# A hybrid attention layer on one core: token places by residue modulo 16, and far blocks of pattern 16 transposed in place

## The chip, the core and the metric

One core of one Trainium2 chip runs the whole layer. The metric is device time in microseconds (us) from start to end of one execution. Besides the timed runs there is one execution taken by the hardware profiler; the rows shown further down come from it. TensorE (PE) multiplies matrices and transposes 128x128 blocks, VectorE (DVE) and ScalarE (ACT) work on elements, GpSimd (POOL) as well but not on PSUM, and SyncE (SP) issues all transfers from one queue, in order.

## What is computed

x has 2048 tokens of 1024 channels. The layer normalises x, projects it with `w_in` (1024 x 4096), runs two groups of channels, and projects their gated outputs back:

```python
h = rmsnorm(x, norm_pre_g)
z = jnp.einsum('bsd,de->bse', h, w_in)
q, k, v, g_attn, c_h, c_b, c_c, g_conv = jnp.split(z, cuts, axis=-1)
...
for window, dilation in ((128, 1), (512, 4), (2048, 16)):
    o_i, lse_i = dilated_window_attn(q, k, v, window, dilation)
...
mix_w = jax.nn.softmax(jnp.stack(lses, axis=0), axis=0)
attn_out = sum(mix_w * outs) * jax.nn.silu(g_attn)
conv_out = c_b * causal_depthwise_conv(c_c * c_h, conv_w) * jax.nn.silu(g_conv)
y = jnp.einsum('bse,ed->bsd', concat(attn_out, conv_out), w_out)
x = x + rmsnorm(y, norm_post_g)
```

There are 12 attention heads of 64 channels, with rotary q and k. Each has three patterns: the last 129 keys, every 4th key back to 512, every 16th key back to 2048, each query seeing 129 keys of a pattern at most. The convolution group has 256 channels and three taps.

## The kernel before

**Stages.** Tokens come in four chunks of 512 (b = 0 to 3). `x_chunk` transposes x on TensorE against an identity, splits the result into a high and a low part (every large product is three matmuls: high x high, high x low, low x high; L848 to L850), and writes it to DRAM. Then 32 units follow, 8 groups of projection columns times 4 chunks: a convolution unit for group 0 and for group 7, and in between `attn_unit` for six pairs of heads (p = 0 to 5). After them the output product takes 8 quarters of 256 tokens, each with 7 forms and 7 products (L1008 to L1010) of a Strassen scheme.

**Places on chip.** A chunk's 512 tokens lie by residue modulo 4: place = 128 r + j for token 4 j + r. `KK` holds the keys as 4 residues x all chunks. Pattern 4 and pattern 16 are computed together, as "kind 4": for a residue r, 128 queries against the keys of the same residue in all chunks up to b (`score4`, L631). In the chunks b - 1 and b a mask takes both patterns; in the chunks before those (the far blocks, c < b - 1) only keys of the same residue modulo 16 count, every 4th of a block, and the mask sets all others to a probability of zero. Pattern 1 is "kind 1": four blocks of 128 consecutive tokens per chunk (`score1`, L659), for which the queries are copied to token order (`Q1`, GpSimd L582) and the keys are read in runs of 32.

**From scores to outputs.** VectorE adds the mask and takes the minimum in one pass out of PSUM (L638, L666), ScalarE takes the exponential and the row sums (L642, L670). A product with v needs keys on partitions, so `probs` transposes the probabilities, four blocks at a time: TensorE into a PSUM bank of ring `st` (L684), ScalarE copies the high part to `pt` (L689), VectorE subtracts for the low part (L690), and TensorE multiplies with v (L703). `gather` adds the halves of the outputs. Row sums of kind 1 go through DRAM (`ed`) to change their order; so does v (`vd`), for kind 1. The two kinds' mixing weights go through DRAM too (`ad`, L788, then broadcast back to `ab`, L791) and multiply the outputs (L807, L808, GpSimd L809).

**What sets the order.** Every operation is handed to a planner (`Plan`) with a duration, a priority and its reads and writes. The planner runs through time, gives each engine the ready operation of lowest priority number, hands out the slots of rings, and emits the instructions of each engine in the order so found. Each engine works its list strictly in that order. It allows for a delay between engines: a long one before TensorE uses another engine's result, a short one between ScalarE and VectorE.

**The output product.** `mixed` loads 128 tokens of one residue modulo 4, 4 x 128 channels, from DRAM; `sums` adds such tiles; `form` splits the sum into a high part (ScalarE, L976) and a low part (VectorE, L977), 56 times each. In `x_chunk`, token order in a chunk was set once, by loading rows 4 apart; `store` writes rows 4 apart.

## Time and profile before

| What | Value |
|---|---|
| Median of 3 runs | 1218.33 us (1218.25 to 1221.13) |
| The profiled execution | 1222.89 us, span 1220.8 us |
| TensorE busy | 1201.8 us, 98% of the span |
| VectorE busy | 916.0 us, 75% |
| ScalarE busy | 717.9 us, 59% |
| GpSimd busy | 260.1 us, 21% |
| Granted TensorE clock | 0.994 |
| One pair of heads, steady | 141 us |

The span is from the first to the last instruction of the profiled execution, whose own time is 2.1 us longer. In rows by line, "L690 DVE TENSOR_TENSOR pt<-st,pt 128x512 ... x204 | 136.1, 686 | 46.8 <-ACT ..." reads: line, engine, operation, what it writes and reads, shapes, count, total busy us, mean ns of one, then the idle time just before them and who ended it. PEld is the loading of the stationary operand, which overlaps PE. A matmul's mean there is its latency through the pipe, so the spacing of matmuls is read from the chain of waits instead, where "829.17 0.87 PE st L684 x8" is a start, a length and a count. Rows that give three durations (673/696/1770) are minimum, median and maximum in ns.

### The profile page before, as it was taken

Reading aid. Unit: us, or ns where it says so; the run is one execution under the profiler, and the core shown is the slowest. Engines: PE = TensorE matmul, PEld = TensorE weight load, DVE = VectorE, ACT = ScalarE, POOL = GpSimd, SP = SyncE. Lnnn points to the kernel's source line nnn. Section 1 sums busy time; section 2 is a strip of 40 time slices with the busy share of each in tenths; the row PEclk is TensorE's granted clock in tenths of the full one; section 3 lists DMA queues with packets and bytes.
Section 4 is the critical chain, followed back from the end, with each engine's and each line's share of the span. In section 5 each row is a group of like instructions: output and inputs, shape, how many; then the busy total and the mean of one; then the engine's idle time right before and its main releaser. Section 6 shows DMA issues by size and latency. Waiting matters only on the chain.

```text
span 1220.8 us, 20955 instructions
## 1 busy us (share of the span) xinstructions
PE 1201.8 (98%) x6856; PEld 993.4 (81%) x6856; DVE 916.0 (75%) x2287; ACT 717.9 (59%) x1874; POOL 260.1 (21%) x212
## 2 busy tenths in 40 slices
PE   8999999999999999999999999999999999999997
PEld 6888888888878888788887888788888888777886
DVE  5556477877777787787788867787877759988876
ACT  6533447767557676576667676486676553454443
POOL 0011123322322232222332223222323113000000
PEclk9999999999999999999999999999999999999999
DMA  9989777766777657766877748767678779555452
GB/s 342 343 317 338 269 232 236 234 205 200 240 252 245 205 182 261 240 184 209 260 223 254 243 119 269 232 234 248 199 233 280 213 229 302 174 163 175 136 181 86
DMA packets 155884, 280.39 MB, mean 230 GB/s; under 512 B 31872, under 2 KB 90368, under 8 KB 155776
## 3 DMA queue, kind: packets, MB, share of 16 engines
q1 hardware_dynamic: 155776, 279.06, 69.6%
q8 instruction: 54, 0.88, 0.3%
q14 instruction: 54, 0.44, 0.1%
HBM read 215.36 MB, written 51.05 MB: 218 GB/s over the span
## 4 chain that ended last, share of the span: by engine, by line
PE 84%; DVE 8%; DMA 3%; ACT 2%; issue 1%; SPq 1%; DVEq 0%; ACTq 0%
PE z L848 16%; PE z L850 16%; PE z L849 16%; PE st L703 8%; PE st L684 7%; PE st L631 4%; PE st L659 3%; PE st L1010 2%; PE st L1008 2%; PE st L1009 2%; DMA rp<-rp 1%; PE z L1008 1%; PE z L1010 1%; PE z L1009 1%; ACT p L642 1%
## 5 line engine op out<-in xcount | busy, mean ns | idle before, releaser
L848 PE MATMUL z<-xt,w 128*128 128x512 f32 x960 | 397.1, 414 | 0.0
L850 PE MATMUL z<-xt,w 128*128 128x512 f32 x960 | 377.7, 393 | 0.0
L849 PE MATMUL z<-xt,w 128*128 128x512 f32 x960 | 376.4, 392 | 0.0
L850 PEld LDWEIGHTS z<-xt,w 128*128 128x128 f32 x960 | 180.5, 188 | 40.3
L848 PEld LDWEIGHTS z<-xt,w 128*128 128x128 f32 x960 | 181.2, 189 | 32.7 <-issue 3.4
L849 PEld LDWEIGHTS z<-xt,w 128*128 128x128 f32 x960 | 181.5, 189 | 25.8
L690 DVE TENSOR_TENSOR pt<-st,pt 128x512 fp32r<-128x512 f32 x216 | 142.3, 679 | 48.1 <-ACT pt L689 46.2
L642 ACT ACTIVATE p<-p,sm 128x128 f32<-128x128 f32 (+3 forms) x192 | 105.9, 555 | 73.2 <-DVE sm L638 72.9
L689 ACT CAST pt<-st 128x512 fp32r<-128x512 f32 x216 | 120.0, 579 | 36.0 <-PE st L684 34.1
L703 PEld LDWEIGHTS st<-pt,v 128*128 128x128 f32 x852 | 121.5, 190 | 18.2 <-DVE pt L690 4.9
L703 PE MATMUL st<-pt,v 128*128 128x256 f32 x852 | 133.1, 287 | 2.0 <-DVE pt L690 1.9
L684 PE MATMUL st<-cst,p 128*128 128x128 f32 x852 | 123.1, 275 | 2.4 <-DVE sm L638 1.0
L723 DVE TENSOR_TENSOR uu<-st,uu 64x256 f32<-64x256 f32 x192 | 80.0, 421 | 57.1 <-ACT uu L722 53.5
L684 PEld LDWEIGHTS st<-cst,p 128*128 128x128 f32 x852 | 100.6, 141 | 22.8 <-issue 3.2
L752 POOL TENSOR_TENSOR uu<-uu 128x512 f32<-128x512 f32 x48 | 72.4, 1509 | 209.1 <-DVE uu L723 207.4
L638 DVE CUSTOM_DVE_ANT_0 p<-st,cst 128x128 f32<-128x128 f32 (+3 forms) x192 | 81.8, 487 | 46.7 <-PE st L631 46.4
L721 ACT COPY uu<-st 64x256 f32<-64x256 f32 x192 | 70.2, 368 | 58.7 <-PE st L703 52.3
L670 ACT ACTIVATE p<-p,e 128x256 f32<-128x256 f32 (+1 forms) x192 | 94.9, 499 | 12.4 <-DVE e L666 12.3
L562 POOL TENSOR_TENSOR rp<-rp,cs 128x512 f32<-128x512 f32 x24 | 35.3, 1472 | 225.7 <-DMA rp<-rp 145.4
L666 DVE CUSTOM_DVE_ANT_0 p<-st,cst 128x256 f32<-128x256 f32 (+1 forms) x192 | 66.8, 411 | 20.5 <-PE st L659 20.4
L562 DVE TENSOR_TENSOR rp<-rp,cs 128x512 f32<-128x512 f32 x72 | 55.9, 791 | 23.4 <-DMA rp<-rp 23.0
L722 ACT COPY uu<-st 64x256 f32<-64x256 f32 x192 | 69.6, 367 | 3.2 <-DVE uu L723 0.4
(320 smaller groups left out, 1842.7 us busy)
## 6 DMA issues: line engine op xcount, KB each, us to landing
xt<-xt SPq DMA_DIRECT2D x256, 512.0 KB
cs<-t SPq DMA_DIRECT2D x28, 768.0 KB
raw<-in_w_in SPq DMA_DIRECT2D x59, 256.0 KB
rp<-rp SPq DMA_DIRECT2D x192, 64.0 KB
vd<-v SPq DMA_DIRECT2D x96, 128.0 KB
v<-vd SPq DMA_DIRECT2D x24, 512.0 KB
ab<-ad SPq DMA_DIRECT2D x48, 256.0 KB
mix<-g SPq DMA_DIRECT2D x32, 256.0 KB
```

The source lines that it names most:

```text
L562: add(e, dur, pr, lambda o=o, a=a, i=i, eng=eng: eng.tensor_tensor(o.ap, a.ap, cs.ap[:, i], op=ALU.mult), r=[cs], w=[o], port=True)
L638: add("DVE", dvet(w) + 0.01, pr + URG, lambda h=h, r=r, P4=P4: vec.tensor_tensor_reduce(P4.ap[:, r, 0:w], ps[h].ap[:, (r - r0) * w:(r - r0 ...
L642: add("ACT", actt(w) + 0.19, pr, lambda h=h, r=r, P4=P4: act.activation(P4.ap[:, r, 0:w], P4.ap[:, r, 0:w], AF.Exp, bias=s4(0, h)[:, r:r + ...
L670: add("ACT", actt(256 - lo[g]) + 0.19, pr, lambda h=h, g=g, P1=P1: act.activation(P1.ap[:, g, lo[g]:], P1.ap[:, g, lo[g]:], AF.Exp, bias=E ...
L684: nc.tensor.transpose(ps.ap[:, i * 128:(i + 1) * 128], pp.ap[:, a, c * 128:(c + 1) * 128], ident)
L689: add("ACT", actt(m * 128, True), pr + URG, lambda: act.copy(pt.ap[:, :m, 0, :], p4()), r=[ps], w=[(pt, 0)])
L690: add("DVE", dvet(m * 128), pr + URG, lambda: vec.tensor_tensor(pt.ap[:, :m, 1, :], p4(), f(pt.ap[:, :m, 0, :]), op=ALU.subtract), r=[ps, ...
L703: mm(dst, v, pt.ap[:, i], start=s, stop=e)
L723: add("DVE", dvet(256), pr + URG, lambda: vec.tensor_tensor(cols(a, lo), o()[lo:lo + 64, 0], cols(a, lo), op=ALU.add), r=[O], w=[(a, (h, h ...
L848: mm(z.ap, w.ap[:, 0, js], xt.ap[:, 0], start=kt == 0, stop=False)
L849: mm(z.ap, w.ap[:, 0, js], xt.ap[:, 1], start=False, stop=False)
L850: mm(z.ap, w.ap[:, 1, js], xt.ap[:, 0], start=False, stop=kt == KT - 1)
```

## The change

A chunk's place is now 128 r + 32 s + a for token 16 a + 4 s + r: within a residue modulo 4, the places of one residue modulo 16 are 32 neighbours. In `x_chunk` the rows of x are loaded as before, and TensorE transposes against a permuted identity (`perm`) that puts the tokens in these places. The tables, masks, shifts of the convolution and all views follow. `KK` is 16 residues x all chunks; `score4` reads it in runs of 32, `score1` in runs of 8. `Q1`, v and E reach the token order of pattern 1 (now a permuted one within its 128) by other views and transfers, of the same count for v and E. The mixing weights take four transfers to `ad` instead of one. The forms of the output product put the tokens back in order: `cells` reads them with a step of 32 elements (L976 and L977, then L1009 and L1010).

In a far block, queries and keys of one residue modulo 16 are now a 32x32 square on the diagonal, and everything else is zero. VectorE's transpose turns each 32x32 square of a tile in place, which for such a block is the whole transpose. So `probs` becomes `parts` and `times`: the far blocks are transposed by VectorE in place (L699), copied by ScalarE and subtracted by VectorE (L701) out of SBUF into `pt`, without TensorE and PSUM; the other blocks go as before. `times` multiplies all blocks of half the outputs in one go.

```diff
-    order = np.arange(C).reshape(128, 4).T.reshape(-1)
+    order = np.arange(C).reshape(32, 4, 4).transpose(2, 1, 0).reshape(-1)
...
+    perm = np.ascontiguousarray(ident[place].T)
...
-                    nc.tensor.transpose(ps.ap[:, i * 128:(i + 1) * 128], xn[i].ap[:, kt * 128:(kt + 1) * 128], ident)
+                    nc.tensor.transpose(ps.ap[:, i * 128:(i + 1) * 128], xn[i].ap[:, kt * 128:(kt + 1) * 128], perm)
...
-        add("DVE", 0.25, pe, lambda: vec.tensor_copy(u.ap[:, 0:2, 1:], u.ap[:, 4:6, 0:127]), r=[(u, 1)], w=[(u, 2)])
+        add("DVE", 0.25, pe, lambda: vec.tensor_copy(u.ap[:, 0:2, 32:], u.ap[:, 4:6, 0:96]), r=[(u, 1)], w=[(u, 2)])
+        add("DVE", 0.15, pe, lambda: vec.tensor_copy(u.ap[:, 0:2, 1:32], u.ap[:, 4:6, 96:127]), r=[(u, 1)], w=[(u, 3)])
...
-                               KK[j][lo:lo + 64, r, 0:w], start=x == 0, stop=x == 2)
+                               KK[j][lo:lo + 64, 4 * r:4 * r + 4, 0:w // 4].rearrange("p s (c a) -> p c s a", a=32), start=x == 0, stop=x == 2)
...
-                            keys = kk[:, :, k0 + 32:k0 + 64] if lo[g] else kk[:, :, k0:k0 + 64].rearrange("p r (c j) -> p c r j", c=2)
+                            keys = kk[:, :, k0 + 8:k0 + 16] if lo[g] else kk[:, :, k0:k0 + 16].rearrange("p x (c a) -> p c x a", c=2)
...
+        def parts(h, kind, blk, far=False):
+            pt, m, pp = Tok(pt_r), len(blk), P[h, kind]
+            tiles = sorted({a for a, _ in blk})
+            if far:
+                def src():
+                    return pp.ap[:, tiles[0]:tiles[-1] + 1, 0:(b - 1) * 128]
+                def dst(l):
+                    return pt.ap[:, :m, l].rearrange("p (a c) q -> p a c q", c=b - 1)
+                def cut(a):
+                    return a.rearrange("p a (c q) -> p a c q", q=128)
+                add("DVE", dvet(m * 128) + 0.05, pr, lambda: vec.transpose(src(), src()), w=[(pp, a) for a in tiles])
+                add("ACT", actt(m * 128), pr + URG, lambda: act.copy(dst(0), cut(src())), r=[(pp, a) for a in tiles], w=[(pt, 0)])
+                add("DVE", dvet(m * 128), pr + URG, lambda: vec.tensor_tensor(dst(1), cut(src()), f(dst(0)), op=ALU.subtract),
+                    r=[(pp, a) for a in tiles] + [(pt, 0)], w=[(pt, 1)], port=True)
...
+                if kind == 4 and b > 1:
+                    where = {}
+                    for half in range(2):
+                        rs = range(2 * half, 2 * half + 2)
+                        if b == 3 or half == 0:
+                            where.update(parts(h, 4, [(r, c) for r in (rs if b == 3 else range(4)) for c in range(b - 1)], True))
+                        where.update(parts(h, 4, [(r, c) for r in rs for c in (b - 1, b)]))
+                        times(h, 4, {ac: v for ac, v in where.items() if ac[0] in rs}, O[half])
...
-        add("DMA", 0.5, pr, lambda: nc.sync.dma_start(
-            ad.rearrange("c g f -> g c f"), ar.ap.rearrange("p a b -> p (a b)")), r=[ar], w=[ak], land=2.0)
+        for r in range(4):
+            add("DMA", 0.5, pr, lambda r=r: nc.sync.dma_start(
+                ad[:, r].rearrange("c s a -> s c a"), ar.ap[:, r]), r=[ar], w=[ak + (r,)], land=2.0)
...
-    add("DMA", 0.5, -158.5, lambda: nc.sync.dma_start(ident, consts[:, 0:128]), w=["cst"])
+    add("DMA", 0.5, -158.5, lambda: nc.sync.dma_start(cst[:, 0:256], consts[:, 0:256]), w=["cst"])
...
-            return m.ap.rearrange("p a c -> p (a c)").rearrange("p (e l t) -> p e l t", e=4, l=2)[:, :, l]
+            return m.ap.rearrange("p a c -> p (a c)").rearrange("p (e l a s) -> p e l a s", e=4, l=2, s=4)[:, :, l]
...
-            return t.ap.rearrange("p (e t) -> p e t", e=4)
+            return t.ap.rearrange("p (e s a) -> p e a s", e=4, s=4)
```

The planner finds a new order for all engines. Two places carry the prediction, both in chunk 3 of a pair of heads. On TensorE, p = 2, the first blocks of probabilities that are multiplied with v (`v_171` to `v_174` are the four chunks' v, `pt` the split probabilities, `p_182` and `p_183` the probabilities of the two heads, `cst` the identity). Before:

```order
L703 MATMUL st_118<-pt_190,v_173 128x2x128
L684 MATMUL st_117<-cst,p_182 128x128 x4
L684 MATMUL st_121<-cst,p_183 128x128 x4
L703 MATMUL st_119<-pt_191,v_174 128x2x128
L703 MATMUL st_119<-pt_191,v_171 128x2x128
L703 MATMUL st_119<-pt_191,v_172 128x2x128
```

Now:

```order
L668 MATMUL st_119<-kk_167,q_170 128x256
L730 MATMUL st_117<-pt_189,v_174 128x2x128
L730 MATMUL st_117<-pt_189,v_171 128x2x128
L730 MATMUL st_117<-pt_191,v_172 128x2x128
L730 MATMUL st_117<-pt_191,v_173 128x2x128
```

One half of a head's outputs is now multiplied in one run, its far blocks out of `pt_189`, its near ones out of `pt_191`, after the scores of pattern 1; the transposes between such runs are half as many. On VectorE, p = 1, the masks of pattern 4 and 16 (L638, now L647, each followed by the reading of its minimum) and what follows. Before:

```order
L638 ISA p_182,sm_162<-st_120,cst 128x512
L638 ISA sm_162 128x1
L638 ISA p_183,sm_162<-st_118,cst 128x512
L638 ISA sm_162 128x1
L690 TENSOR_TENSOR pt_189<-st_121,pt_189 128x4x128
L690 TENSOR_TENSOR pt_190<-st_119,pt_190 128x4x128
```

Now:

```order
L647 ISA p_183,sm_162<-st_120,cst 128x512
L647 ISA sm_162 128x1
L699 STREAM_TRANSPOSE p_182<-p_182 128x2x256
L699 STREAM_TRANSPOSE p_183<-p_183 128x2x256
L701 TENSOR_TENSOR pt_189<-p_182,pt_189 128x4x128
L647 ISA p_182,sm_162<-st_118,cst 128x512
```

The transposes stand in VectorE's queue ahead of the masks of the next scores, and they wait for ScalarE's exponentials of the same tiles. In the whole program TensorE has 708 transposes of probabilities where it had 852. After the last product with v, 222 projection matmuls stand before the first matmul of the output product where 192 stood.

More of the change, by code (lines that the diff above doesn't have):

```diff
@@ L582, in attn_unit @@
             add("POOL", poolt(C) / 2, pr, lambda l=l: pool.tensor_copy(
-                Q1.ap[:, l].rearrange("p (g r j) -> p g r j", g=4, r=4), Q.ap[:, l].rearrange("p (r g j) -> p g r j", g=4, r=4)),
+                tokens(Q1.ap[:, l]), rows(Q.ap[:, l])),
                 r=[(Q, l)], w=[(Q1, l)])
@@ L696, in pv, with times @@
+        def times(h, kind, where, O):
+            def pv():
+                for (a, c), (pt, i) in sorted(where.items()):
+                    dst = O.ap.rearrange("p (l q) -> p l q", l=2)[:, :, (a % 2) * 128:(a % 2 + 1) * 128]
                     if kind == 4:
@@ L704, in probs @@
             vs = [V2[p * NB + c] for c in range(b + 1)] if kind == 4 else [V1[p * NB + c] for c in range(max(b - 1, 0), b + 1)]
-            for half in range(2):
-                part = [(i, ac) for i, ac in enumerate(blk) if ac[0] // 2 == half]
-                if part:
-                    attn_last.append(add("PE", mmt(256) * len(part), pr, lambda part=part: pv(part), r=[(pt, 0), (pt, 1)] + vs, w=[O[half]]))
+            attn_last.append(add("PE", mmt(256) * len(where), pr, pv,
+                                 r=[(pt, l) for pt in {pt for pt, _ in where.values()} for l in range(2)] + vs, w=[O]))
         UU = {}
@@ L745, in attn_unit @@
                 O = [Tok(st_r), Tok(st_r)]
-                for i in range(0, len(bl), 4):
-                    probs(h, kind, bl[i:i + 4], O)
+                if kind == 4 and b > 1:
[6 more added lines that the diff above has]
+                        times(h, 4, {ac: v for ac, v in where.items() if ac[0] in rs}, O[half])
+                else:
+                    for i in range(0, len(bl), 4):
+                        where = parts(h, kind, bl[i:i + 4])
+                        for half in range(2):
+                            part = {ac: v for ac, v in where.items() if ac[0] // 2 == half}
+                            if part:
+                                times(h, kind, part, O[half])
                 for half in range(2):
```

99 lines of the change are left out of this document (46 added, 53 removed).

## Prediction, made before the changed kernel ran

> **What bounds the kernel now.** I read the first part of the page, then the busy time by stage, then the waits of TensorE.
>
> ```profile
> span 1220.8 us, 20955 instructions
> PE 1201.8 (98%) x6856; PEld 993.4 (81%) x6856; DVE 916.0 (75%) x2287; ACT 717.9 (59%) x1874; POOL 260.1 (21%) x212
> ```
>
> A busy share can hide matmuls that merely wait in the pipe, so the stages come next: one pair of heads in the steady middle (750 to 891 us), the change to the output product (1010 to 1100), the output product itself (1100 to 1200). The columns are length, then busy time and instructions of PE, PEld, DVE, ACT, POOL, then granted clock and DMA share.
>
> ```profile
> 750.00:891.00 141.00, 140.13 (x874) 116.76 (x875) 110.81 (x296) 93.68 (x263) 39.11 (x32) 1.00 0.71 226
> 1010.00:1050.00 40.00, 40.00 (x178) 33.13 (x177) 39.11 (x67) 14.02 (x25) 8.84 (x6) 1.00 0.76 254
> 1050.00:1100.00 50.00, 47.60 (x195) 36.79 (x194) 43.39 (x87) 24.39 (x51) 2.95 (x2) 0.97 0.52 171
> 1100.00:1200.00 100.00, 99.74 (x428) 79.75 (x427) 82.18 (x175) 45.30 (x102) 0.00 (x0) 1.00 0.48 159
> ```
>
> And what TensorE waited for, in the attention stage (125 to 1010 us) and after it, with total, count and longest:
>
> ```profile
> PE st L703 <- DVE pt L690: 1.9, 1, 1.9
> ...
> PEld st L703 <- DVE pt L690: 4.9, 10, 2.3
> ...
> PE st L1008 <- ACT xt L976: 1.8, 1, 1.8
> PE z L1010 <- DVE xt L977: 0.6, 1, 0.6
> PE z L1008 <- ACT xt L976: 0.3, 1, 0.3
> ```
>
> TensorE's queue is the kernel's clock. Nothing in attention holds it for longer than these few microseconds of 885, so a TensorE instruction taken out there is taken out of the time, as long as the other engines keep up. VectorE is next: 110.8 of 141 us per pair of heads, 82 of 100 in the output product, 39 of 40 just before that.
>
> **What the change takes away.** TensorE transposed every 128x128 block of probabilities. The change takes the far blocks of pattern 16 off it: per head 4 in chunk 2 and 8 in chunk 3, so 12 x 2 heads x 6 pairs = 144 of the 852 instructions of L684. The mean of 275 ns in the grouped rows is latency in the pipe; what a transpose costs the queue is in the chain:
>
> ```profile
> L684 PE MATMUL st<-cst,p 128*128 128x128 f32 x852 | 123.1, 275 | 2.4 <-DVE sm L638 1.0 <-DVE e L666 0.7 <-ACT p L642 0.6
> ...
> 829.17 0.87 PE st L684 x8
> 830.05 0.47 PE st L703 x4
> ...
> 830.75 0.23 PE z L849
> ```
>
> 0.87 / 8 = 0.109 us, and 144 x 0.109 = 15.7 us. The products with v (L703, 852) and the scores stay as many as they were. This is the whole gain, 2.6 us for each pair of heads.
>
> **What it adds in attention.** 36 groups of four blocks now go VectorE transpose, ScalarE copy, VectorE subtract. Rows for their prices:
>
> ```profile
> L785 DVE STREAM_TRANSPOSE t<-pa 128x128 f32<-128x128 f32 x24 | 7.5, 312 | 0.8
> L690 DVE TENSOR_TENSOR pt<-st,pt 128x512 fp32r<-128x512 f32 x204 | 136.1, 686 | 46.8 <-ACT pt L689 45.0
> L690 DVE TENSOR_TENSOR pt<-st,pt 128x384 fp32r<-128x384 f32 x12 | 6.6, 552 | 1.3 <-ACT pt L689 1.1
> L573 DVE TENSOR_TENSOR kk<-rp,kk 128x512 fp32r<-128x512 f32 x24 | 19.4, 810 | 0.0
> ```
>
> The trace has the transpose at 128 elements only. At 512 it lies between 0.686 (a two-input operation of that size) and 4 x 0.312 = 1.25 us; growing like L690, by (686 - 552) / 128 = 1.05 ns an element, it is 0.312 + 384 x 0.00105 = 0.72, which I take, the row of the operation itself carried on at the slope of its neighbour. 36 x 0.72 = 25.8 us. The subtract now reads two operands in SBUF; L573, which does that and meets GpSimd, shows 0.810 for 0.686: 36 x 0.124 = 4.5 us. Together 30.3, or 5.0 per pair of heads: VectorE goes from 110.8 in 141 to 115.8 in 138.4 us, 84%. So VectorE stays off the bound on average, and the cost is waits. The present chain (transpose on TensorE, copy, subtract) shows 1.9 + 4.9 us over 216 groups, 0.031 each. The new one crosses between ScalarE and VectorE three times instead of once, and a transpose that waits for a late exponential holds all that is queued behind it on VectorE, the mask operations (L638) of the next scores among them. I take double, 0.063 x 36 = 2.3 us given back. The bounds are 0 and, if the longer first step shows each time, 36 x (0.72 - 4 x 0.109) = 10.2.
>
> Edits that I cost at little: the scores' keys. Before, the first pattern's scores read runs of 32 elements, pattern 16's whole rows; with equal columns (chunk 1, 256) they took the same:
>
> ```profile
> 317.97 1.63 PE st L631 x24
> ...
> 323.22 1.64 PE st L659 x24
> ```
>
> So breaking rows into 32s is free for TensorE; runs of 8 I take as free too (a rival below). VectorE likewise reads runs of 32 as it reads whole rows (L807 against L808, below). The multiplications that now run over whole rows therefore gain nothing. The weights' way to DRAM is four transfers instead of one:
>
> ```profile
> L788 SPq DMA_DIRECT2D ad<-t x24: 583/592/660, 168.3 to 1013.8; - x24
> ...
> DVE uu L807 <- DMA ab<-ad: 1.4, 1, 1.4
> ...
> L807 DVE TENSOR_TENSOR uu<-uu,ab x24: 673/696/1770, 179.0 to 1027.1; 128x512 f32<-128x512 f32 x24
> L808 DVE TENSOR_TENSOR uu<-uu,ab x24: 674/682/1780, 183.4 to 1030.5; 128x512 f32<-128x512 f32 x24
> ```
>
> Three issues more put the weights back by at most 3 x 0.59 = 1.8 us, and move every later transfer in SyncE's queue by as much. L807 waited once in 24, so other work covers it; with that cover gone, VectorE would idle 24 x 1.8 = 43 us, 7 per pair of heads out of its 22.6 idle, still no TensorE term. The round trips of v and E keep five transfers each. Eight more short copies in the convolution cost under 8 x 0.28 us of VectorE (row L512). The first constants to load double, and TensorE's wait for them may grow by up to itself; I take 0.2 us.
>
> ```profile
> L512 DVE COPY u<-u x8: 278/282/286, 40.1 to 1053.5; 128x254 f32<-128x254 f32 x8
> ...
> PE st L442 <- DMA cst<-in_consts: 0.5, 1, 0.5
> ```
>
> **What it adds in the output product.** The 56 forms (8 quarters x 7) read their tokens back in natural order: the innermost step goes from 1 to 32 elements, in the copy (L976) and the subtract (L977). No row has that at this size. The nearest are 8-element operations: L769, L770 and L778 step 4 elements in one source, L771 and L779 are the same kinds without a step.
>
> ```profile
> L977 DVE TENSOR_TENSOR xt<-uu,xt x33: 677/686/694, 1046.0 to 1203.4; 128x512 fp32r<-128x512 f32 x33
> ...
> L769 DVE TENSOR_TENSOR sm<-ex,sm x24: 149/168/1252, 163.9 to 1010.1; 128x8 f32<-128x8 f32 x24
> L770 DVE TENSOR_TENSOR sm<-sm,ex x24: 171/174/1289, 164.1 to 1010.4; 128x8 f32<-128x8 f32 x24
> L771 DVE TENSOR_TENSOR sm<-sm,sm x24: 151/158/1273, 165.2 to 1011.5; 128x8 f32<-128x8 f32 x24
> L778 DVE TENSOR_TENSOR sm<-sm,ex x24: 154/168/599, 167.0 to 1012.5; 128x8 f32<-128x8 f32 x24
> L779 DVE TENSOR_TENSOR sm<-sm,sm x24: 152/155/1279, 167.0 to 1012.5; 128x8 f32<-128x8 f32 x24
> ...
> 1050.00:1100.00 50.00, 10.07 (x15) 0.97 0.52 171
> 1100.00:1200.00 100.00, 24.58 (x37) 1.00 0.48 159
> ```
>
> The last two rows are L977 alone by stage, 37 in the 100 us of the output product. By medians the step costs up to 174 - 158 = 16 ns over 8 elements, 2.0 ns each or 1.02 us a form; by minima the three pairs differ by -2 (L769 to L771), 20 and 2, a mean of 0.83 ns each or 0.43 us; the least is nothing. I take 0.43. VectorE's slack is 17.8 us over 37 forms, 0.48 each. So VectorE would be 98% busy and TensorE still sets the pace, barely. What an in-order queue loses at that load: nothing if all the slack can be used, 56 x 0.1 = 5.6 us if a fifth of it can't; I take the middle, 2.8. ScalarE has 55 of 100 us free and covers its own copies. The step before is safer: 15 forms (1050 to 1100) add 6.5 us to VectorE, which had 6.6 idle there, and by the instruction order 222 projection matmuls instead of 192 now stand between the last product with v and the first output matmul, 30 x 0.23 = 6.9 us more for VectorE's backlog. That could also remove the 2.7 us of waits after 1010; I leave that to the low end.
>
> The Trainium skill's "Vector Engine (DVE) Microarchitecture Reference" (5.2, Measured stream behaviour on trn2) speaks against this edit: a port streams at full rate only over runs of at least two adjacent words, and one source that hops every element takes 1.73 ns a column for 1.054. An estimate from that page is 0.35 us more a form, inside the slack, and the sum would be the same or up to 2.8 us better. No run here shows its rate at 512 elements.
>
> **The sum.** -15.7 + 2.3 + 0.2 + 2.8 = -10.4 us. The profiled execution took 1222.9 us (span 1220.8 and 2.1 around it), 4.6 above the median of 1218.33; on it the sum gives 1212.5, and on the median 1207.9.
>
> **Rivals.** First, VectorE becomes the bound of the output product (slower). Place: L977, 56 times. If a stepped element costs the 2.0 ns of the medians, a form takes 1.02 us more, 0.54 above the slack: 56 x 0.54 = 30 us, in place of the 2.8. -15.7 + 2.3 + 0.2 + 30 = +17, 1235. It cancels the gain from 0.48 + 13.2 / 56 = 0.72 us more a form, that is L977 at 1.4 us. For it: the medians. Against it: two of three minima show nothing. Chance that it takes over at all 0.22, half of it past the point of no gain.
>
> Second, attention waits take the place of the transposes: 10.2 for 2.3 us gives -2.5, 1215.8. For it: VectorE already waits 45 us for the copy before L690. Against it: TensorE lost only 0.031 us a group through that. Chance 0.12.
>
> Third, the first pattern's scores slow down: 576 matmuls read runs of 8. The chain's 1.64 us for 24 is 0.068 each; at twice that, 576 x 0.068 = 39 us more, 1247. Against it: 32-element runs cost nothing. Chance 0.05.
>
> Fourth, the transposes were not on the path at all: no change, about 1218. TensorE's rows speak against it. Chance 0.05.
>
> **The numbers.** The forecast keeps 0.56. Low end: no cost anywhere and the 2.7 us of waits gone, 1218.3 - 15.7 - 2.7 = 1199.9, so 1200. High end: forms at 0.74 us more, 56 x 0.26 = 14.6, and 2.3 and 0.2, +1.4 or 1219.7, and a little of what lies beyond: 1221. About 0.3% (3.7 us) is what a measurement of this kernel can tell from no change. Faster by more: 0.56, 0.11 of the first rival and 0.03 of the second, 0.70. Within it: 0.02 of the first, 0.09 of the second, 0.05 of the fourth, 0.16. Slower: 0.09 and 0.05, 0.14.
>
> **What would show it.** Right: 708 transposes on TensorE at 0.109 us in the chain, a pair of heads in some 138.8 us, 36 VectorE transposes near 0.72, the form subtract near 1.1, TensorE still over 99% in the middle of the output product. Wrong: TensorE waiting for VectorE in chunks 2 and 3, L977's successor above 1.4 us with VectorE full from 1100 on, or 24 score matmuls of the first pattern well over 1.64.

## The result, and the profile after

The changed kernel takes 1229.29 us (median of 6 runs, 1224.77 to 1231.03) where the kernel before takes 1218.58 beside it (6 runs, 1216.28 to 1221.13): a ratio of 1.0079, 95% interval 1.0058 to 1.0100, so 0.8% slower. 1207.9 was forecast, and 1229.29 lies outside the range of 1200 to 1221. The profiled execution took 1226.19 us, 3.1 below the median of its kernel (that of before was 4.3 above); sums are therefore made from medians here, and profiles only show where. All times here are of executions whose mean granted clock was 0.979 or more; one execution, of the kernel below whose planner knows the longer durations, had 0.653 and took 1670 us, and is left out.

The page of the changed kernel:

```profile
span 1224.4 us, 20804 instructions
PE 1193.9 (98%) x6712; PEld 985.3 (80%) x6712; DVE 945.4 (77%) x2331; ACT 747.1 (61%) x1874; POOL 263.0 (21%) x212
```

TensorE has its 144 instructions less, and the span is longer all the same. Where, the stages tell, in the same stretches as in the prediction:

```profile
750.00:891.00 141.00, 139.05 (x848) 115.60 (x847) 109.93 (x301) 95.04 (x264) 38.49 (x32) 0.99 0.74 222
1010.00:1050.00 40.00, 39.06 (x171) 31.54 (x170) 34.16 (x49) 18.72 (x27) 11.09 (x7) 1.00 0.64 202
1050.00:1100.00 50.00, 44.55 (x181) 34.26 (x180) 41.27 (x75) 28.07 (x45) 0.00 (x0) 0.97 0.44 143
1100.00:1200.00 100.00, 92.23 (x390) 72.09 (x389) 85.26 (x163) 56.73 (x94) 0.00 (x0) 1.00 0.41 138
```

The pair of heads looks as forecast: by the first scores of kind 4 (L640), the four steady pairs from 288.9 to 845.5 us took 139.2 us each. In the output product (last row) TensorE does 390 matmuls where it did 428, and is idle for 7.8 us of 100. The grant of its clock is full there, and no engine is full either. The first matmul of the output product and the last start of the same group, before:

```profile
L1008 PE MATMUL st<-kk,xt x14: 389/394/505, 1051.5 to 1194.2; 128*128 128x512 f32 x14
```

and after:

```profile
L1041 PE MATMUL st<-kk,xt x12: 393/395/694, 1039.6 to 1197.4; 128*128 128x512 f32 x12
```

So the changed kernel reaches the output product 11.9 us earlier, and has lost all of it, and more, by the eighth quarter. Attention gained; the output product gave it back.

The parts of the change, in the groups of the changed kernel's instructions:

```profile
L730 PEld LDWEIGHTS st<-pt,v 128*128 128x128 f32 x852 | 117.5, 190 | 13.6 <-DVE pt L714 2.3 <-issue 1.1 <-DVE pt L701 1.0
...
L1009 ACT CAST xt<-uu 128x512 fp32r<-128x512 f32 x36 | 40.3, 1140 | 34.1 <-DVE uu L930 32.1 <-PE z L882 1.9
L1010 DVE TENSOR_TENSOR xt<-uu,xt 128x512 fp32r<-128x512 f32 x36 | 39.8, 1113 | 17.0 <-ACT xt L1009 17.0
L668 PE MATMUL st<-kk,q 64*128 64x256 f32 x540 | 44.9, 308 | 3.4 <-DVE sm L647 3.4
L701 DVE TENSOR_TENSOR pt<-p,pt 128x512 fp32r<-128x512 f32 x36 | 25.5, 707 | 1.1
L699 DVE STREAM_TRANSPOSE p<-p 128x512 f32<-128x512 f32 x36 | 24.2, 697 | 8.4 <-ACT p L651 8.4
```

and in its chain, in attention:

```profile
315.27 1.64 PE st L640 x24
...
320.54 1.83 PE st L668 x24
...
325.02 0.87 PE st L708 x8
```

The VectorE transpose takes 0.70 us (0.72 was said), the subtract out of SBUF 0.707 (0.810), the stepped subtract 1.11 (1.1). A transpose on TensorE still costs 0.87 / 8 = 0.109. Two things stand out: 24 score matmuls of pattern 1 take 1.83 us for 1.64, and ScalarE's stepped copy takes 1.14 us for 0.615 (its mean in the kernel before), which no step of the prediction priced. The copy's row before:

```profile
L976 ACT CAST xt<-uu 128x512 fp32r<-128x512 f32 x33 | 19.6, 615 | 23.6 <-DVE uu L898 23.5
```

TensorE's waits in the output product (total, count, longest):

```profile
PE st L1041 <- ACT rp L1048: 4.3, 5, 1.0
PE z L1041 <- ACT rp L1048: 3.9, 4, 1.0
PE z L1041 <- ACT g L1048: 2.8, 2, 1.8
PE z L1043 <- DVE xt L1010: 2.3, 1, 2.3
```

L1048 is `keep`, ScalarE's copy of a finished PSUM bank, without which the next product has no bank. My first theory after the result read this row literally: `keep` stands in ScalarE's in-order queue behind stepped copies that take 1.14 us instead of 0.62. The chain of the same stretch shows more:

```profile
1137.93 1.01 ACT w L1009
1138.94 0.02 issue
1138.96 1.08 DVE w L1010
1140.04 0.02 issue
1140.07 0.70 DVE uu L930
1140.77 0.02 issue
1140.79 2.16 ACT xt L1009 x2
```

Copy, subtract, the next sum, the next copies: over these 5 us the chain isn't on TensorE at all but goes back and forth between ScalarE and VectorE, and each of its stepped pieces takes 1.01 to 1.08 us where the copy took 0.62 and the subtract 0.69 before.

### The profile page after: what moved, and what is told of

It reads as the page before. It is cut to its first block, busy times and chain, and to the rows that moved or that the text cites. A ratio compares the mean times of both kernels' runs of the same rounds, so it can differ in the third digit from the quotient of the medians.

```text
span 1224.4 us, 20804 instructions
## 1 busy us (share of the span) xinstructions
PE 1193.9 (98%) x6712; PEld 985.3 (80%) x6712; DVE 945.4 (77%) x2331; ACT 747.1 (61%) x1874; POOL 263.0 (21%) x212
## 4 chain that ended last, share of the span: by engine, by line
PE 70%; DVE 12%; DMA 7%; ACT 5%; issue 3%; SPq 2%; POOL 0%; DVEq 0%; ACTq 0%
PE z L880 15%; PE z L882 15%; PE z L881 15%; PE st L730 7%; PE st L708 5%; PE st L640 3%; PE st L668 3%; ACT xt L1009 2%; DVE xt L1010 2%; DMA vd<-v 2%; DMA ed<-e 1%; PE st L880 1%; PE st L882 1%; PE st L881 1%; PE st L446 1%
## 5 line engine op out<-in xcount | busy, mean ns | idle before, releaser
L730 PEld LDWEIGHTS st<-pt,v 128*128 128x128 f32 x852 | 117.5, 190 | 13.6 <-DVE pt L714 2.3
L714 DVE TENSOR_TENSOR pt<-st,pt 128x512 fp32r<-128x512 f32 (+1 forms) x180 | 117.1, 674 | 11.6 <-ACT pt L713 10.3
L730 PE MATMUL st<-pt,v 128*128 128x256 f32 x852 | 124.6, 285 | 1.0 <-DVE pt L714 0.9
L713 ACT CAST pt<-st 128x512 fp32r<-128x512 f32 (+1 forms) x180 | 98.7, 579 | 17.7 <-PE st L708 16.2
L647 DVE CUSTOM_DVE_ANT_0 p<-st,cst 128x128 f32<-128x128 f32 (+3 forms) x192 | 81.9, 486 | 30.2 <-PE st L640 29.8
L708 PE MATMUL st<-cst,p 128*128 128x128 f32 x708 | 100.0, 275 | 0.4 <-DVE uu L748 0.3
L790 POOL TENSOR_TENSOR uu<-uu 128x512 f32<-128x512 f32 x48 | 66.9, 1393 | 136.3 <-DVE uu L748 126.7
L708 PEld LDWEIGHTS st<-cst,p 128*128 128x128 f32 x708 | 83.4, 141 | 13.9 <-issue 1.6
```

What stands on the lines that cost most here:

```text
L647: add("DVE", dvet(w) + 0.01, pr + URG, lambda h=h, r=r, P4=P4: vec.tensor_tensor_reduce(P4.ap[:, r, 0:w], ps[h].ap[:, (r - r0) * w:(r - r0 ...
L708: nc.tensor.transpose(ps.ap[:, i * 128:(i + 1) * 128], pp.ap[:, a, c * 128:(c + 1) * 128], ident)
L713: add("ACT", actt(m * 128, True), pr + URG, lambda: act.copy(pt.ap[:, :m, 0, :], p4()), r=[ps], w=[(pt, 0)])
L714: add("DVE", dvet(m * 128), pr + URG, lambda: vec.tensor_tensor(pt.ap[:, :m, 1, :], p4(), f(pt.ap[:, :m, 0, :]), op=ALU.subtract), r=[ps, ...
L730: mm(dst, v, pt.ap[:, i], start=s, stop=e)
```

## The experiments

All ratios are to the kernel before, run beside the kernel on the same chip, with 95% intervals; its medians there were 1218.68 to 1219.75.

### The parts of the change

**The layout without the in-place transposes**: the flag that sends the far blocks to VectorE is left out, so TensorE transposes all 852 blocks.

```diff
-    where.update(parts(h, 4, [... for c in range(b - 1)], True))
+    where.update(parts(h, 4, [... for c in range(b - 1)]))
```

> The changed kernel with the far blocks transposed by TensorE again: the new places with all their costs, without the in-place transposes. If these are worth what the milestones say (15.7 us less the waits they add): 1229.3 + 12 = about 1241. If VectorE's part costs attention as much as TensorE saves: 1229.

1242.94 us, ratio 1.0194 (1.0177 to 1.0211). The layout alone costs 23.9 us, and the in-place transposes on top of it bring 1242.94 - 1229.29 = 13.6. The prediction had -15.7 + 2.3 = -13.4 for them. That half of it was right; the layout was wrong.

**The stepped forms alone, in the kernel before**: `view` and `cells` of the change, nothing else.

> The kernel before, with nothing changed but the step of 32 in the forms' reading (the output rows then come out in another order within 128; the work is the same). If the stepped reading alone makes the loss of the output product: 1218.6 + 17 = about 1236, a quarter at 22 us. If the changed kernel's order makes it: 1219 to 1222.

1246.41 us, ratio 1.0224 (1.0209 to 1.0239), +27.3. Its forms:

```profile
L976 ACT CAST xt<-uu 128x512 fp32r<-128x512 f32 x33 | 36.6, 1131 | 31.4 <-DVE uu L898 31.2
L977 DVE TENSOR_TENSOR xt<-uu,xt 128x512 fp32r<-128x512 f32 x33 | 35.5, 1083 | 15.3 <-ACT xt L976 15.3
```

The same two durations as after the change, and a cost of the same kind: it belongs to the step, not to the new order in attention.

**Pattern 1's keys in runs of 32**: the scores read as many keys in whole runs of 32, which are other keys.

```diff
-    keys = kk[:, :, k0 + 8:k0 + 16] if lo[g] else kk[:, :, k0:k0 + 16].rearrange("p x (c a) -> p c x a", c=2)
+    keys = kk[:, 0:4, sl] if lo[g] else kk[:, 0:8, sl]
```

> The changed kernel, but the first pattern's scores read 256 keys in runs of 32 instead of 8 (other keys, so other scores; the work is the same). In the chain of the changed kernel 24 such matmuls take 1.83 us where they took 1.64. If runs of 8 cost TensorE that: back to 1.64, 24 x 0.19 = 4.5 us, 1225. If something else made them longer: 1229.

1224.65 us (9 runs), ratio 1.0046 (1.0029 to 1.0062): 4.6 us less than the changed kernel; the two intervals overlap, so the size rests on the chain as well. Its group of these matmuls:

```profile
L668 PE MATMUL st<-kk,q 64*128 64x256 f32 x540 | 40.9, 290 | 2.4 <-DVE sm L647 2.4
```

290 ns again, as before the change. By the chain, 0.19 us more for 24 makes 576 / 24 x 0.19 = 4.6 us. Runs of 8 are not free.

**Token order by the transfers instead**: forms as before, and x and the output move in four pieces of 32 rows each.

```diff
-    xr.ap, x[b * C + i:(b + 1) * C:4, dl]
+    xr.ap, x[b * C:(b + 1) * C].rearrange("(a s i) d -> i s a d", s=4, i=4)[i][:, :, dl]
```

> The changed kernel, but its forms read whole rows again (step 1), and the output rows are put in order by the transfers of x and of the result instead. The profile of the changed kernel shows a quarter of the output product at 22.0 us where it was 19.5, about 17 us over seven quarters, while the stages before it end 11.9 us earlier than before. If the stepped reading of the forms causes that loss: L976's successor back at 0.62, L977's at 0.69, a quarter at 19.5, and 1229.3 - 17 = about 1212, faster than the kernel before by 0.5%. If the loss comes from the order of the instructions or from attention: 1226 or more.

A miss: 1256.34 us, ratio 1.0309 (1.0283 to 1.0334). VectorE now waits for the tiles of the mixed outputs:

```profile
DVE uu L930 <- DMA uu<-mix: 39.0, 8, 8.1
```

The stepped reads are gone, but VectorE waits 39 us in eight waits for transfers, so the run says nothing on them. The kernels below do, without new transfers.

### Which of the two stepped reads

Three kernels undo the step in both, in ScalarE's copy, or in VectorE's subtract, each by an edit of this form (here the copy; `flat` and `row` are `view` and `cells` without the step):

```diff
-    act.copy(view(m, 0), cells(t))
+    act.copy(flat(m, 0), row(t))
```

Neither steps:

> The changed kernel with neither engine stepping in the forms (the output rows then come out in another order within 128; the work is the same): the fourth corner beside the changed kernel and the two that stepped on one engine only, 1213.3 and 1214.0. If the two steps add up, it lies as far below those as they lie below the changed kernel, near 1198. If one stepping engine is nearly free and only both together hold TensorE up: 1209 to 1212.

ScalarE's copy doesn't step:

> The changed kernel, but ScalarE's copy in the forms reads whole rows (step 1) and only VectorE's subtract steps (the low parts then belong to other tokens; the work is the same). Theory: TensorE waits for a PSUM bank whose copy stands behind two 1.14 us copies in ScalarE's queue; then most of the 17 us come back, 1213 to 1217, and TensorE's waits for L1048's successor go. Rival: VectorE's 1.11 us subtracts fill VectorE; then 1226 or more.

VectorE's subtract doesn't step:

> The mirror of the run before: ScalarE's copy in the forms steps by 32, VectorE's subtract reads whole rows (high and low part then belong to different tokens; the work is the same). Theory (ScalarE's queue holds back the copies that free TensorE's banks): of the 17 us lost in the output product only the few that the copy's plain reading left are gained, 1224 to 1228, and TensorE still waits for L1048's successor some 13 us in all. Rival (either engine's longer work will do): 1218 or less.

The last four columns are from 1060 to 1190 us of each kernel: TensorE's matmuls, what VectorE and ScalarE were busy, and how long VectorE's subtracts in the forms waited for the copy. The row of the changed kernel:

```profile
1060.00:1190.00 130.00, 116.79 (x483) 90.15 (x482) 108.94 (x197) 73.06 (x117) 0.00 (x0) 0.99 0.43 144
```

| Which read steps | Median, us | Ratio | Matmuls in 130 us | VectorE | ScalarE | VectorE's waits for copies |
|---|---|---|---|---|---|---|
| neither | 1208.19 | 0.9910 (0.9885 to 0.9934) | 552 | 104.73 | 58.53 | 10.3 |
| VectorE's | 1213.33 | 0.9957 (0.9942 to 0.9971) | 523 | 117.08 | 55.09 | 8.9 |
| ScalarE's | 1214.01 | 0.9965 (0.9950 to 0.9980) | 520 | 99.56 | 77.92 | 23.3 |
| both (the change) | 1229.29 | 1.0079 (1.0058 to 1.0100) | 483 | 108.94 | 73.06 | 17.7 |

Without the steps the change comes to 1208.2, near the forecast (4.6 for the runs of 8 in place of the 2.8 for the forms). One step costs 5.1 or 5.8 us, both 21.1: nearly twice their sum. The traces show the same operations in the same order in all four kernels, on TensorE, on VectorE and on ScalarE, so the order is no part of this difference. This fells the theory of ScalarE's queue, by which ScalarE's step alone had to keep nearly all of the loss. It also fells the first rival as it was put, VectorE's work as the bound. VectorE's work per matmul is the same in the second and the fourth row (117.08 / 523 = 0.224 and 108.94 / 483 = 0.226 us), and the loss 5 and 21. The sizes, where only the subtract steps:

```profile
L1016 DVE TENSOR_TENSOR xt<-uu,xt 128x512 fp32r<-128x512 f32 x36 | 39.9, 1123 | 8.5 <-ACT xt L1015 8.3
L1015 ACT CAST xt<-uu 128x512 fp32r<-128x512 f32 x36 | 21.4, 617 | 38.3 <-DVE uu L930 35.9 <-issue 2.4
```

and where only the copy does:

```profile
L1015 ACT CAST xt<-uu 128x512 fp32r<-128x512 f32 x36 | 40.4, 1145 | 24.7 <-DVE uu L930 23.2 <-PE z L882 1.5
L1016 DVE TENSOR_TENSOR xt<-uu,xt 128x512 fp32r<-128x512 f32 x36 | 26.0, 721 | 20.4 <-ACT xt L1015 20.4
```

### Why both together

The waits of the table's last column, before the subtracts into `xt`, for both, VectorE's, ScalarE's and neither:

```profile
DVE xt L1010 <- ACT xt L1009: 14.7, 14, 1.2
DVE xt L1016 <- ACT xt L1015: 7.5, 11, 0.7
DVE xt L1016 <- ACT xt L1015: 18.9, 26, 1.2
DVE xt L1010 <- ACT xt L1009: 7.6, 11, 0.7
```

The forms in `w` add 3.0, 1.4, 4.4 and 2.7. VectorE's work and these waits together fill 126.6, 126.0, 122.9 and 115.0 us of 130. Carried by the number of matmuls to TensorE's full pace, 561 in 130 us (a kernel below shows it), that is an estimate of 147, 135, 133 and 117 us. A step in the subtract adds work to VectorE's queue, a step in the copy adds waiting; either alone overruns 130 us by 3 to 5, both by 17. This says where VectorE's time goes. It is not an experiment; those follow.

**Less work for VectorE**: the multiplication by `norm_post_g` in place (24 of 32) is left out.

> The changed kernel without VectorE's multiplication by norm_post_g where it works in place (24 of 32; the output lacks that factor there): 3 x 0.68 = 2.0 us less of VectorE's work a quarter, nothing else. If VectorE's load sets the quarter at 22.0 us: back to 20 or below, 1229.3 - 8 x 2 = about 1213. If a chain of form after form, ScalarE then VectorE, sets it: 1226 or more.

1231.18 us, ratio 1.0097 (1.0076 to 1.0119). It gives nothing back, at a like granted clock neither (at 0.996, one execution of each took 1229.71 and 1229.51 us). From 1060 to 1190 us VectorE works 105.08 us for 108.94 and waits 20.2 us for copies for 17.7: work taken out came back as waiting. VectorE's work alone is not what holds TensorE.

**The planner is told**: `actt(C) + 0.6` and `dvet(C) + 0.5` for the forms.

> The changed kernel with true durations given to the planner for the forms: 0.6 us more for ScalarE's copy, 0.5 more for VectorE's subtract. Nothing else; the order that the planner finds changes. If the loss is one of order (a bank's copy behind two long copies), at least half of the 17 us comes back: 1215 to 1220. If the engines' capacity is gone: 1227 or more.

1227.45 us (3 runs), ratio 1.0074 (1.0047 to 1.0101): not clear of the changed kernel, and far from the half of the loss that the theory of order asked for. Its granted clock was a little lower (0.990 to 0.993), which may hide a few us: the changed kernel's own executions went from 1224.77 us at 0.998 to 1231.03 at 0.992. But TensorE's waits after 1090 us are others:

```profile
PE z L1043 <- DVE xt L1010: 3.9, 2, 1.9
PE st L1043 <- DVE xt L1010: 3.5, 2, 2.0
```

With another order TensorE waits for the forms themselves rather than for `keep`. The row of a wait names the one who came last, not the cause.

**Copies and subtracts in halves**: VectorE can start on the first half while ScalarE copies the second.

```diff
-    add("ACT", actt(C), pr, lambda: act.copy(view(m, 0), cells(t)), ...)
-    add("DVE", dvet(C), pr, lambda: vec.tensor_tensor(view(m, 1), cells(t), f(view(m, 0)), ...), ...)
+    for k in (0, 2):
+        e = slice(k, k + 2)
+        add("ACT", actt(C // 2), pr, lambda e=e: act.copy(view(m, 0)[:, e], cells(t)[:, e]), r=[t], w=[(m, k)])
...
+        add("DVE", dvet(C // 2), pr, lambda e=e: vec.tensor_tensor(view(m, 1)[:, e], ...), r=[t, (m, k)], w=[(m, k + 1)], port=True)
```

> The changed kernel with each form's stepped copy and stepped subtract cut in two halves, so that VectorE starts on the first half while ScalarE copies the second: more instructions and some 0.07 us more work for either engine a form, but a shorter way through each form, by about 0.5 us. If the way through the forms sets the quarter: 22.0 falls below 21 and the time to 1222 or less. If VectorE's load or the order does: 1230 or more.

1220.60 us (10 runs), ratio 1.0016 (1.0001 to 1.0032): 8.7 us come back although both engines have more to do (by the means below 2 x 667 and 2 x 622 ns a form, for 1140 and 1113).

```profile
L1011 ACT CAST xt<-uu 128x256 fp32r<-128x256 f32 x62 | 37.8, 667 | 20.2 <-DVE uu L930 17.3 <-PE z L882 2.9
L1014 DVE TENSOR_TENSOR xt<-uu,xt 128x256 fp32r<-128x256 f32 x62 | 36.5, 622 | 6.8 <-ACT xt L1011 6.2
```

So VectorE's and ScalarE's load is not what counts here; the length of the way through a form fits, though the planner's order differs too.

**Tiles of their own for the sums.** In a quarter, the sum S2 overwrites the tile of S3, S1 that of A22, S4 that of A12, so a sum waits until the copy and the subtract of the form before it have read the tile. The control adds a sixth tile to the five that hold a quarter's loads; the other kernel then also gives S3 a tile of its own, puts S1 into A11's and S4 into S3's.

```diff
-    mr_r = uu_r + list(g_r)[2:]
+    mr_r = uu_r + list(g_r)[2:] + list(raw_r)[2:]
...
-    sums("S3", a21, a11, a21, ALU.subtract)
-    form("S3", a21)
-    sums("S2", a21, a22, a21, ALU.subtract)
+    s3 = Tok(mr_r)
+    sums("S3", s3, a11, a21, ALU.subtract)
+    form("S3", s3)
+    sums("S2", a21, a22, s3, ALU.subtract)
```

> The changed kernel with six tiles instead of five for the loaded quarters of the output product (the sixth is taken from the six that the residual of x goes through). The changed kernel took 1229.3. If the long forms hurt because the next quarter's four tiles can only be loaded once this quarter's forms have let go of theirs, a sixth tile gives back several us: 1220 to 1225. If the tiles themselves are not short, and what counts is that a sum which overwrites a tile waits for the copy and the subtract of the form before it, or only the order in the engines' queues, nothing moves: 1227 to 1231.

> As the run with six tiles, and in addition no sum overwrites a tile whose form is still being read: S3 gets a tile of its own, S1 goes into the tile of A11, S4 into that of S3. The work on every engine is the same. If the way through a quarter is long because each sum waits for the copy and the subtract of the form before it, that way loses two forms of some 2.2 us in each of 8 quarters, of which the 2.5 us per quarter that were lost are to be had at most: 1212 to 1222. If only the order of ScalarE's and VectorE's queues counts, whatever the tiles, it stays within 2 us of the run with six tiles.

The control: 1229.38 us, ratio 1.0090 (1.0070 to 1.0110), no change. With tiles apart: 1221.11 (12 runs), ratio 1.0024 (1.0009 to 1.0038), 8.3 us less at the same work on every engine. In its output product:

```profile
1060.00:1190.00 130.00, 119.92 (x494) 93.73 (x493) 115.05 (x211) 77.86 (x124) 0.00 (x0) 0.97 0.43 142
```

VectorE gets more done in the same time (115.05 us, 108.94 in the changed kernel), and TensorE with it (494 matmuls for 483).

**Both cures, and the tiles where nothing steps**:

> The changed kernel with tiles of their own for the sums (1221.1) and with each copy and subtract in two halves as well (alone 1220.6, for 1229.3). Both shorten the way through a quarter, the halves by letting VectorE start on the first half while ScalarE copies the second. If the length of that way is what is left of the loss, the two add up in good part: 1212 to 1217. If the tiles were all of the way and the rest is load or queue order, the halves add only work: 1220 to 1224.

> Tiles of their own for the sums, and neither the copy nor the subtract steps (their output rows stand in the order of the places, so the rows of a chunk come out in another order than the reference's). With the tiles overwritten that took 1208.2. If separate tiles help only by cutting a way that the stepped reads made too long, nothing is left to gain here: 1206 to 1210. If they help for another reason, they gain about 8 us here too: 1200.

Both cures: 1220.60 us, ratio 1.0005 (0.9991 to 1.0019), so at most 1 to 2 us beyond either (by ratios; the medians and the overlapping intervals show no difference), not 8. Its output product, and that of the second kernel of this pair:

```profile
1060.00:1190.00 130.00, 119.35 (x498) 93.39 (x497) 120.01 (x258) 81.71 (x169) 0.00 (x0) 0.99 0.44 144
1060.00:1190.00 130.00, 130.00 (x561) 104.83 (x560) 102.21 (x223) 59.90 (x133) 0.00 (x0) 1.00 0.48 156
```

VectorE is busy 120.01 us for 498 matmuls, 0.241 each; at the pace of the second kernel, whose TensorE never waited there, it would be needed for 135 us of 130. By that estimate, VectorE's load stands in the way of more. Where nothing steps, separate tiles still bring 4.1 us: 1204.10, ratio 0.9880 (0.9861 to 0.9898, which just overlaps the interval without them). So about half of their 8.3 us goes with the step; the rest they bring anyway.

**Work moved to GpSimd**, which is idle in the output product: the copies of the forms, or the sums.

```diff
-    add("ACT", actt(C), pr, lambda: act.copy(view(m, 0), cells(t)), ...)
+    add("POOL", 1.1, pr, lambda: pool.tensor_copy(view(m, 0), cells(t)), ...)
```

> The changed kernel with the forms' stepped copies on GpSimd, which does nothing in the output product, in place of ScalarE; the subtracts stay stepped on VectorE. The way through a form keeps its length if GpSimd takes about as long as ScalarE's 1.14 us. If the loss comes from TensorE's banks waiting behind long copies in ScalarE's queue and from the two queues holding each other up, it goes in good part: 1212 to 1218. If it is the length of the way through the forms, whichever engine's queue it stands in, nothing is gained: 1225 to 1231, or more if GpSimd is slower.

> The changed kernel with the sums of the output product (four per quarter, 0.69 us on VectorE) on GpSimd, at some 1.4 us each by its other operations of this size. Copies and subtracts step as before. The way through a quarter gets longer by 0.7 us a sum, but a sum no longer stands behind the long subtracts in VectorE's queue. If the two queues holding each other up is the loss: 1214 to 1222. If the length of the way is: 1232 or more.

Copies: 1252.47 us, ratio 1.0258 (1.0235 to 1.0281). ScalarE's queue holds no copies of forms any more, and it is 23 us slower than the changed kernel:

```profile
L1010 DVE TENSOR_TENSOR xt<-uu,xt 128x512 fp32r<-128x512 f32 x37 | 51.0, 1391 | 21.2 <-POOL xt L1009 21.0
L1009 POOL CAST xt<-uu 128x512 fp32r<-128x512 f32 x37 | 41.5, 1134 | 109.7 <-DVE uu L930 104.4 <-PE st L1042 2.8 <-issue 2.6
```

The copy takes as long as on ScalarE (1134 ns), but the mean of VectorE's subtract goes from 1113 to 1391. The mean mixes two kinds, as minimum, median and maximum tell:

```profile
L1010 DVE TENSOR_TENSOR xt<-uu,xt x37: 1021/1110/1958, 1035.8 to 1238.5; 128x512 fp32r<-128x512 f32 x37
```

Of all 56 subtracts, the 32 with GpSimd idle beside them took 1.02 to 1.12 us, as in the changed kernel; 20 took 1.82 to 1.96 us, and beside each of these a GpSimd copy ran through about half of its time. The granted clock was lower as well, 0.984 on average for 0.995, which an estimate (1.1% of 1250 us) puts at up to 14 of the 23 us. So the test is not a clean one: it shows that freeing ScalarE's queue is not enough, not what the longer subtract alone costs. Sums: 1233.20 us, ratio 1.0118 (1.0100 to 1.0136), 3.9 slower, with an interval that touches that of the changed kernel. Its output product:

```profile
1060.00:1190.00 130.00, 114.26 (x459) 86.59 (x459) 92.24 (x165) 69.44 (x112) 29.94 (x23) 0.97 0.41 134
```

VectorE is busy for 92 us of 130, 17 less than in the changed kernel, and TensorE does 459 matmuls for 483: each sum takes 1.39 us on GpSimd for 0.69, so the way is longer. Less load with a longer way doesn't gain and probably loses; more load with a shorter way (the halves) gains.

### A version that beats both

The step can go where fewer wait for it. GpSimd's last multiplication in `attn_unit` writes its result in token order, the convolution's last operation on VectorE does the same, and the forms read plainly.

```diff
-    pool.tensor_tensor(gs.ap, a4.ap, gs.ap, op=ALU.mult)
+    pool.tensor_tensor(natural(a1.ap), placed(a4.ap), placed(gs.ap), op=ALU.mult)
```

> A correct version without stepped reading in the output product: GpSimd's last multiplication of each attention unit (and VectorE's of each convolution unit) writes the tokens in natural order, stepping 4 elements, so that the forms read whole rows. 32 stepped operations off the bound take the place of 112. If nothing else was lost: the output product starts 12.5 us earlier than before and keeps its old 19.5 us a quarter, 1219.0 - 12.5 = about 1206.5. If GpSimd's stepped writes hold up the mixing: 1212 or more.

1211.18 us (6 runs), ratio 0.9941 (0.9921 to 0.9960). The stepped write takes GpSimd no longer, 1442 ns for 1507 at L842 in the changed kernel:

```profile
L849 POOL TENSOR_TENSOR uu<-uu,g 128x512 f32<-128x512 f32 x24 | 34.6, 1442 | 1.9
```

It is not free for the whole: the kernel in which nothing steps took 1208.19, 3.0 us less (the intervals overlap). Up to 1040 us, TensorE here waits 7.9 us for the subtract of the probabilities, and 1.5 in the kernel in which nothing steps:

```profile
PE st L732 <- DVE pt L716: 7.9, 10, 1.7
PE st L730 <- DVE pt L714: 1.5, 4, 0.7
```

The planner's order differs between the two, so whether the write or the order brings these waits is open.

With tiles of their own for the sums as well:

> The kernel in which GpSimd writes the mixed outputs in token order, so that no form steps (1211.2), with tiles of their own for the sums and a sixth tile. Where nothing stepped, separate tiles went with 4 us (1204.1 for 1208.2): 1207 expected. If that difference was within the spread, 1211.

1207.23 us (6 runs), ratio 0.9915 (0.9893 to 0.9938), 0.85% faster than the kernel before, the best found that keeps the reference's order of rows; it is again 3.1 us above its counterpart without any step (1204.10). In its output product TensorE never waits:

```profile
1100.00:1200.00 100.00, 100.00 (x432) 80.62 (x432) 74.84 (x166) 42.88 (x97) 0.00 (x0) 1.00 0.46 147
```

## Why the prediction was wrong, point by point

- **What bounds the kernel, and the transposes: right.** TensorE's queue is the clock in attention. The in-place transposes with their waits came to -13.6 us by medians, -13.4 was said. The second rival (waits in attention, 10.2) and the fourth (no effect) did not happen: in the whole of attention TensorE's weight loads waited 1.0 us for L701, and its matmuls longest for a mask, 3.4 us in all (L647).
- **"Runs of 8 I take as free too": wrong.** They cost 4.6 us, 12% on 576 matmuls. What was shown free was a run of 32; a run of 8 was carried over from it with no row of its own. The third rival had the mechanism, at eight times the price (39 us), and a chance of 0.05.
- **The output product, 2.8 us: the step that failed.** It was 21.1. Its size for one operation was good: 0.43 us more a subtract was taken and 0.40 (medians, 1086 for 686) to 0.43 measured. The estimate of 0.35 from the Trainium skill's "Vector Engine (DVE) Microarchitecture Reference" (5.2) was a little low. The prediction's load on VectorE was good too: at 0.226 us per matmul, 561 matmuls would need 127 of 130 us, 97%, and 98% was said. What failed was to turn load into time. "ScalarE has 55 of 100 us free and covers its own copies" is a statement on capacity, and so is VectorE's slack of 0.48 a form. But a form is a way: sum on VectorE, copy on ScalarE, subtract on VectorE, each waiting for the one before, in queues that work strictly in order. ScalarE's copy, which got no price at all, lengthens that way by 0.53 us, more than the subtract's 0.4. VectorE's slack was spent twice: on the longer subtracts, and on waiting for the longer copies, 17.7 us of 130 where it waited 8.9 when only the subtract stepped.
- **The first rival** had the right place (L977's successor) and the right sign, with 0.22, but the wrong mechanism and a wrong condition. It asked for a subtract of over 1.4 us and a full VectorE. The subtract was 1.11, VectorE worked 85 us of 100, and TensorE starved. Only with its waits for the copies counted in was VectorE's queue nearly full, and these waits were not in the rival.
- **What would show it**: of the signs of being right, 708 transposes at 0.109, a pair of heads in 139.2 us (138.8 was said), 0.70 for the transpose and 1.11 for the subtract all came; TensorE over 99% in the output product did not. Of the signs of being wrong only the runs of 8 came. No sign had been named for what happened, because the way through both engines was in none of the rivals.

By medians: -13.6 for the transposes, +4.6 for the runs, +21.1 for the forms is +12.1, where +10.7 was measured. The 1.4 left is within the spread of these medians.

**What stays open.** Shown: half of the loss comes only when both reads step, with the same order on every engine. It is not VectorE's work alone. Another order of the same operations (from the longer durations, or from a sixth tile) moved the time by less than 2 us. Copies ahead of `keep` don't explain it, because ScalarE's step alone costs 5.8. Shortening the way gives 8 to 9 us back, by halves or by tiles apart. Not settled: how the 21 us divide. The overwritten tiles account for some 4 beyond what separate tiles bring anyway. For the rest, two in-order queues that hold each other up, with VectorE needed for 97% of the time at TensorE's full pace and waiting for copies besides, is the account that fits the four traces, but it is argued: no run changed a wait alone. Why both cures together still leave 12 us (1220.60 for 1208.19) is open too; VectorE's load is only an estimate for it.

## What to carry to other kernels

Before an operation is called covered because its engine is half idle, follow one piece of work through all engines and ask what its way becomes: two engines that take turns can lose more when both get slower than the two losses alone add up to (here 5.1 and 5.8 us, and 21.1 together). A change of layout has to be priced at every reader, each with its own run length or step; the reader that got no price was the one that cost most. If one operation must take the awkward step, look for an engine that takes it at no longer duration, and measure the whole: GpSimd's write stepped without getting longer, and the kernel kept all but 3 of the 21 us.

## What the runs showed of the hardware

- A step of 32 fp32 elements in an SBUF source takes a 128x512 operation on ScalarE from 0.62 to 1.14 us, a two-input one on VectorE from 0.69 to 1.09 (medians), and a copy on GpSimd comes to 1.13 with it.
- Where GpSimd makes the copies, VectorE's stepped subtract took 1.02 to 1.12 us with GpSimd idle, and 1.82 to 1.96 us when a GpSimd copy ran beside it through half of its time.
- GpSimd writing in steps of 4 elements (two inputs, 128x512) takes 1.44 us (mean); the unstepped ones of the changed kernel in attention 1.39 to 1.51.
- TensorE's moving operand in runs of 8 fp32 elements: 1.83 us for 24 matmuls of 256 columns, 1.64 in runs of 32.
- VectorE transposes the 32x32 squares of a 128x512 tile in place in 0.70 us.
